# One core, a hybrid decoder layer: weight sums split in place, an earlier norm of the convolution group, a later compression of the values, another order of the last rows

## The chip, the cores and the metric

One core of a Trainium2 chip runs the kernel in one launch. The metric is device time in microseconds: of the kernel before three runs took 1395.77 in the median (1395.15 to 1396.4). Everything read from a trace comes from one profiled execution of 1392.82 us, whose span from the first to the last instruction is 1390.9 us.

## The reference

The layer is one block of a decoder with 1024 tokens, width 1024, all in float32:

```python
n1 = rms_norm(h, g_mix); proj = n1 @ w_in          # columns: conv (3 x 512), q, 6 x k/v, gates
y_conv = b_gate * causal_dwconv(c_gate * x_in, w)  # width-3 convolution, 512 channels
kc = compress_kv(k_cmp); vc = compress_kv(v_cmp)   # blocks of 32 tokens, step 16: silu(flat @ w1) @ w2
y_attn = native_sparse_attention(...)              # compressed + top-8 selected blocks + window of 512, gated
mixed = concat([rms_norm(y_conv, g_gn_conv), rms_norm(y_attn, g_gn_attn)])
h = h + mixed @ w_out
u = causal_dwconv(rms_norm(h, g_ffn) @ w_up, w_ffn_conv)   # 2 x 2816 columns, width 3
h = h + (silu(u_gate) * u_val) @ w_down
h = h + sigmoid(rms_norm(h, g_ple) @ w_ple_gate) * (p @ w_ple_proj)
out = rms_norm(h, g_final)
```

## The kernel before

Activations lie transposed, channels on the partitions and tokens along the free dimension, in tiles of 128 x 1024 called pages (29 of them in the pool). Each float32 operand of a product is split into a high and a low part of type fp32r (split, L99: ACT copies the high part, DVE subtracts for the low part), and each product is three matmuls (mm3, L196 to L199): high with high, high with low, low with high. An operand whose raw data lie in the tile of its low part is split by in_place (L110).

The code is written as generators and loops, and a planner of the framework gives each engine its order: by its own estimate of the times it takes, on each engine, the first instruction in the order of the code that is ready. `behind(later, earlier)` (L203) adds an order between two instructions of one engine without a wait. Tiles are slots of pools; a tile's first writer waits for the last reader of the slot's former tile. Loads are issued from SP's queue, in order.

Weights are named in a list by `plan` (L137; the list is at L289 to L318). `fetch` loads them ahead into raw tiles and `send` splits them; `weights(key)` returns the parts and splits three more ahead. Until the end of attention there are two raw slots (NWR) and eight part slots (NWT), that is four split tiles.

The stages in order:

1. Input products (from L366), the rotary pairs of keys, then the compression: `cmp_proj` makes the 128 columns of the compressed keys (kind 0) and values (kind 1), `stack` (L452) lays them out by transfers from tile to tile, and `compress(kind)` (L464) does 16 x 3 small products with w1, a Silu with a bias, a split, and the product with w2. `queries(g)` (L514) makes two query tiles of 96 matmuls altogether and can call a function between them. L527 to L532: stack of the keys, queries(0), compress of the keys, stack of the values, queries(1) with the compress of the values between its two tiles. Then the values and gates of the eight token tiles (L547 to L554), with the weights vg0, vg3, vg6.
2. The convolution group (L873 to L900) and its sum of squares `cacc`.
3. Attention by blocks of 128 queries, in the order 3, 7, 6, 5, 4, 2, 1, 0 (L954 to L977). `merge` (L837) deals the steps of several generators out over each other: `selected`, `values`, `finish` for the block, `nearest`, `choose`, `window` for the next. The products of the convolution group with its rows of w_out are filled in between (`conv_out`, L846; 16 half tiles of 12 matmuls, three, five and six of them in blocks 2, 1, 0). For them ych, ycl are the split of yc times its gain; the rstd row crb multiplies the product on DVE (L856), and POOL adds this to a page with x, loaded at L851. `attn_norm(hf)` (L909) norms 512 tokens of the attention group; for the upper half it runs as a whole behind the first merge of block 1.
4. `out_half` (L1006): products of the attention group with w_out for the upper and the lower half, and sums of squares. The rstd of the upper half (norm1, L1100) is taken behind three steps of the lower half.
5. The gated MLP by a scheme of seven products in place of eight: the operands are quarters of the weights and of the activations and sums of them. `up_weights(j)` (L1027) loads the two raw tiles of step j (gate and value columns), and makes the parts: products 1 and 2 use the gate columns, products 6 and 5 their sums t (ut), products 7 and 3 the sums a7 and a3 (us), product 4 a part of the value columns (uv). For the steps 0, 1, 20 and 21 (SUMMED) the sums were made in DRAM during attention, as usum, and are loaded: t into a page, a7 and a3 into two tiles of 512. The parts and raw tiles of this stage lie in a pool of 18 slots ("fp"), opened when attention's pools close. Between the halves and the MLP the embeddings' products (`embed`, L1111) and the splits of the moving operands (`moving`, L1063) run.
6. The down products, the gate of the embeddings, and the end: tokens 0 to 767 stay transposed; `final` (L1385) norms them by a rstd whose sums are a small product, and stores them from POOL's queue. The last two token tiles (`late`, 6 and 7) are turned round and computed in rows: `token_product` and `gated` (L1458), which also multiplies by g_final, and `norm` (L1477), which scales by the rstd, half on DVE and half on ACT, and stores. `rsqrt` (L233) is a root on ACT and a reciprocal on DVE, or, for the names in NEWTON, an iteration of twelve small DVE operations.

Of the kernel before, what the change touches and what calls it, by code (L numbers as in the profile page):

```python
# [9 lines left out]
F32 = mybir.dt.float32  # L10
# [26 lines left out]
def hybrid_layer(ctx: ExitStack, tc: tile.TileContext, xT, pT, w_in, w_vg, w_out, w_up, w_down,  # L37
# [157 lines left out]

    def mm3(ps, wh, wl, mh, ml, start, stop, **more):  # L196
        first = nc.tensor.matmul(ps, wh, mh, start=start, stop=False, **more)  # L197
        nc.tensor.matmul(ps, wh, ml, start=False, stop=False, **more)  # L198
        return first, nc.tensor.matmul(ps, wl, mh, start=False, stop=stop, **more)  # L199
# [33 lines left out]
    def rsqrt(ms, n, name, eng=None):  # L233
# [3 lines left out]
        if name not in NEWTON:  # L237
            rs = small.tile([P, 32], F32, tag="rr", name=name + "rr", bufs=1)[:, 0:f]
            nc.scalar.activation(rs, ms, AF.Sqrt, bias=eps, scale=1.0 / n)
# [53 lines left out]
    plan("c11", c_w1[1], 16 * HD)  # L293
    plan_in(7)
    for a in range(0, KC, 3):
        n = min(3, KC - a) * 280
        plan(f"vg{a}", w_vg[:, a * 280:a * 280 + n], n)
    for j in range(4):
# [165 lines left out]
    def compress(kind, st):  # L464
# [20 lines left out]
        split(w2, w2h, w2l, lo_eng="dve")  # L485
        po = bank(n + "o")
        if kind == 0:
            for q in range(2):
                sl = slice(q * P, (q + 1) * P)
                mm3(po[:, sl], w2h[:, sl], w2l[:, sl], hh, hl, True, True)  # L490
# [14 lines left out]
        else:  # L505
            mm3(po[:, 0:64], hh, hl, w2h[:, 0:64], w2l[:, 0:64], True, True)
            for g in range(NG):
                r = slice(64 * g, 64 * g + 64)
                nc.vector.tensor_copy(vc[r, g, :], po[r, 0:64])

# [3 lines left out]
    def queries(g, between=None):  # L514
        ps = []
        for q in range(2):
            t = pair(f"q{g}{q}")
            proj(weights(f"in{4 + 2 * g + q}"), xm, both(t))
            ps.append(t)
            if between and q == 0:  # L520
                between()
# [8 lines left out]
    compress(0, kst)  # L530
    vst = stack(1, *vc_parts)
    queries(1, lambda: compress(1, vst))  # L532
    cmp_stack.close()
    halves = mix.enter_context(tc.tile_pool(name="halves", bufs=1, side="right"))
# [12 lines left out]
    for i in range(NI):  # L547
        sl = slice(i * P, (i + 1) * P)
        pv = bank(f"pv{i}")
        for k in range(KC):  # L550
            mm3(pv[:, 0:280], xh[k][:, sl], xl[k][:, sl], wvh[k], wvl[k], k == 0, k == KC - 1)
        nc.scalar.activation(vsw[i // 4][:, i % 4, :], pv[:, 0:256], AF.Copy, scale=rstd[:, i:i + 1])
        nc.scalar.activation(gates[:, i], pv[:, 256:280].rearrange("p (h b) -> p h b", b=3), AF.Sigmoid,
                             scale=rstd[:, i:i + 1])  # L554

# [290 lines left out]
    def conv_out():  # L846

        for c in range(KC):
# [3 lines left out]
            for hf in range(2):  # L852
                po = bank(f"oc{c}{hf}")
                proj(w, (ch, cl), lambda _: po, (hf,))
                v = half([P, 512], f"ov{c}{hf}")
                nc.vector.tensor_mul(v, po, crb[:, hs(hf)])  # L856
                nc.gpsimd.tensor_add(t[:, hs(hf)], v, t[:, hs(hf)])
# [51 lines left out]
    def attn_norm(hf, sums=None):  # L909
# [17 lines left out]
        yield  # L927
# [712 lines left out]
```

## Time and profile before

| | us |
|---|---|
| median of three runs | 1395.77 |
| the profiled execution | 1392.82 |
| its span | 1390.9 |
| PE busy | 1342.0 (96%) |
| DVE busy | 949.8 (68%) |
| ACT busy | 640.6 (46%) |
| POOL busy | 209.9 (15%) |
| mean granted TensorE clock | 0.989 |

PE is TensorE's matmul row, DVE VectorE, ACT ScalarE, POOL GpSimd, SP the engine that issues loads. The chain of work that ended last is PE for 87% of the span and DVE for 6%. The granted clock is a share of 2.4 GHz: 1.00 is that, 0.50 is 1.2 GHz. A wait is told with the engine and operation that released it; a release by several is put down to the one that came last.

### The profile page before, as it was taken

What the parts mean: (1) busy time and instruction counts of PE and PEld (TensorE: products, weight loads), DVE (VectorE), ACT (ScalarE), POOL (GpSimd) and SP (SyncE); (2) the same over time, 40 slices, a digit from 0 to 9 for tenths busy, and PEclk for the clock granted to TensorE, in tenths of its full rate; (3) what the DMA queues carried; (4) which work ended last, traced back from release to release, by engine and by line L of the source; (5) the groups of instructions that cost most, each with busy time, mean ns of one, the idle gap of its engine ahead of it and who ended that gap; (6) DMA issues with size and microseconds to landing.
All of it is one profiled execution on the core that took longest, in us unless ns stands there. A gap on an engine that the chain in (4) does not pass through costs nothing.

```text
span 1390.9 us, 17780 instructions
## 1 busy us (share of the span) xinstructions
PE 1342.0 (96%) x6395; PEld 1056.3 (76%) x6395; DVE 949.8 (68%) x1754; ACT 640.6 (46%) x1095; POOL 209.9 (15%) x226
## 2 busy tenths in 40 slices
PE   8989999999999999898999999999999999999995
PEld 6869888865666667686888878888887888888884
DVE  7752333387778785787877788876678776566677
ACT  6222111177767652555434444443345564345443
POOL 0211001233333555000010111110001000000001
PEclk9999999999999999999999999999999999999998
DMA  8473311068787971652376667766568996552434
GB/s 274 106 189 120 104 46 46 20 168 162 175 175 156 258 176 39 212 182 83 106 167 157 179 180 180 176 136 136 139 159 235 321 329 216 174 164 75 145 110 174
DMA packets 105462, 220.74 MB, mean 159 GB/s; under 512 B 9120, under 2 KB 30624, under 8 KB 105376
## 3 DMA queue, kind: packets, MB, share of 16 engines
q1 hardware_dynamic: 79280, 153.30, 34.4%
q0 software_dynamic: 26096, 66.33, 23.6%
q8 instruction: 50, 0.82, 0.3%
q14 instruction: 36, 0.29, 0.1%
HBM read 184.99 MB, written 91.49 MB: 199 GB/s over the span
## 4 chain that ended last, share of the span: by engine, by line
PE 87%; DVE 6%; DMA 2%; issue 2%; SPq 1%; ACT 1%; POOL 0%; DVEq 0%; ACTq 0%; POOLq 0%
PE ua L197 4%; PE ua L198 4%; PE ua L199 4%; PE uc L197 3%; PE uc L198 3%; PE uc L199 3%; PE sy L781 2%; PE d L197 2%; PE d L199 2%; PE d L198 2%; PE da L198 2%; PE da L199 2%; PE da L197 2%; PE wy L781 2%; PE g L197 2%
## 5 line engine op out<-in xcount | busy, mean ns | idle before, releaser
L108 DVE TENSOR_TENSOR a<-a 128x512 fp32r<-128x512 f32 x77 | 51.8, 687 | 31.8 <-ACT a L105 31.7
L1207 ACT ACTIVATE uc<-xg,vec 128x1024 f32<-128x1024 f32 x22 | 25.3, 1152 | 97.1 <-DVE xg L1200 94.2
L105 ACT ACTIVATE a<-a 128x512 fp32r<-128x512 f32 x77 | 47.5, 627 | 47.3 <-DMA a<-asum 24.6
L105 ACT ACTIVATE in_h<-in_r 128x1024 fp32r<-128x1024 f32 (+1 forms) x20 | 20.7, 1036 | 96.2 <-PE cx L198 30.1
L1200 DVE TENSOR_TENSOR xg<-uc,e 128x512 f32<-128x512 f32 x22 | 15.2, 690 | 63.6 <-PE uc L199 63.5
L733 ACT ACTIVATE ps<-ps,stat 128x512 f32<-128x512 f32 (+7 forms) x64 | 49.1, 770 | 11.6 <-DVE stat L744 11.5
L108 DVE TENSOR_TENSOR down_p<-down_r,down_p 128x512 fp32r<-128x512 f32 x55 | 37.2, 687 | 24.6 <-ACT down_p L105 24.5
L197 PE MATMUL d<-a,down_p 128*128 128x512 f32 x132 | 52.1, 395 | 0.0
L199 PE MATMUL d<-a,down_p 128*128 128x512 f32 x132 | 52.1, 394 | 0.0
L198 PE MATMUL d<-a,down_p 128*128 128x512 f32 x132 | 52.0, 394 | 0.0
L198 PE MATMUL da<-a,down_p 128*128 128x512 f32 x132 | 51.9, 394 | 0.0
L197 PE MATMUL da<-a,down_p 128*128 128x512 f32 x132 | 50.6, 395 | 1.3 <-ACT a L105 1.3
L105 ACT ACTIVATE down_p<-down_r 128x512 fp32r<-128x512 f32 x55 | 34.2, 627 | 37.2 <-PE d L199 14.1
L199 PE MATMUL da<-a,down_p 128*128 128x512 f32 x132 | 51.1, 393 | 0.0
L105 ACT ACTIVATE ugh<-ugr 128x1024 fp32r<-128x1024 f32 x22 | 23.3, 1059 | 59.3 <-DMA ugr<-in_w_up_dram 59.3
L108 DVE TENSOR_TENSOR in_l<-in_r,in_h 128x1024 fp32r<-128x1024 f32 (+2 forms) x22 | 25.0, 1140 | 28.1 <-ACT in_h L105 28.1
L1235 POOL DMA_DIRECT2D asum<-ad x11 | 8.4, 764 | 236.7 <-DMA ad<-uc 236.7
L1392 POOL DMA_DIRECT2D out_dram<-h x8 | 4.4, 554 | 258.4 <-DVE h L1391 258.4
L197 PE MATMUL g<-g,pg_h 128*128 128x256 f32 (+1 forms) x128 | 43.4, 339 | 0.0
L198 PE MATMUL g<-g,pg_h 128*128 128x256 f32 (+1 forms) x128 | 43.2, 337 | 0.0
L199 PE MATMUL g<-g,pg_l 128*128 128x256 f32 (+1 forms) x128 | 43.1, 338 | 0.0
L652 ACT ACTIVATE pw<-pw,stat 128x640 f32<-128x640 f32 (+3 forms) x56 | 38.3, 687 | 10.0 <-DVE stat L706 5.8
(763 smaller groups left out, 4503.3 us busy)
## 6 DMA issues: line engine op xcount, KB each, us to landing
asum<-ad POOLq DMA_DIRECT2D x33, 768.0 KB, 8.6
wsum<-in_w_down_dram POOLq DMA_DIRECT2D x6, 2816.0 KB, 20.9
ugr<-in_w_up_dram SPq DMA_DIRECT2D x22, 512.0 KB, 6.9
ad<-uc SPq DMA_DIRECT2D x22, 512.0 KB, 2.9
a<-asum SPq DMA_DIRECT2D x44, 256.0 KB, 5.7
down_r<-wsum SPq DMA_DIRECT2D x44, 256.0 KB, 3.8
in_r<-in_w_in_dram SPq DMA_DIRECT2D x18, 512.0 KB, 7.0
uvr<-in_w_up_dram SPq DMA_DIRECT2D x18, 512.0 KB, 5.6
```

The costliest lines, as they stand in the source:

```text
L105: nc.scalar.activation(hi, x, AF.Copy)
L108: (nc.gpsimd if (lo_eng or lo_of[0]) == "pool" else nc.vector).tensor_sub(lo, x, f32(hi))
L197: first = nc.tensor.matmul(ps, wh, mh, start=start, stop=False, **more)
L198: nc.tensor.matmul(ps, wh, ml, start=False, stop=False, **more)
L199: return first, nc.tensor.matmul(ps, wl, mh, start=False, stop=stop, **more)
L652: nc.scalar.activation(w[:, :b.nw * P], w[:, :b.nw * P], AF.Exp, bias=b.M_W[:, h:h + 1], scale=-1.0, accum_out=b.D_W[:, h:h + 1])
L733: nc.scalar.activation(w[:, :nk], w[:, :nk], AF.Exp, bias=b.M_S[:, h:h + 1], scale=-1.0, accum_out=b.D_S[:, h:h + 1])
L781: m = nc.tensor.matmul(py[64 * g:64 * g + 64, :], vals(n, g), pts[g], start=n == 0, stop=n == nblk - 1)
L1200: nc.vector.tensor_add(xg[:, hi], c, e2)
L1207: nc.scalar.activation(u, xe[:, 0:S], AF.Copy, scale=col(tap))
L1235: nc.gpsimd.dma_start(d[:, 0:3], three(one))
L1392: nc.gpsimd.dma_start(out[k], o)
```

## The change

Five edits. (A) compress becomes a generator with a pause before its second product, whose first matmul is put behind the newest mm3; the keys' second part comes after the first half of the first tile of queries(1), the values' two parts come in the loop over token tiles, at tiles 2 and 4; c11 moves behind vg in the list of weights; the pool of the compression closes after that loop. (B) The convolution group is multiplied by gain and rstd row ahead of the split, so that its output products are added to x by one DVE operation; attn_norm pauses after each of its four tiles, and the upper half's is dealt out over the first merge of block 0. (C) Four steps of the lower half instead of three stand before the upper half's rstd. (D) Summed up-weights are loaded into the low parts and split in place. (E) The rstd of tokens 0 to 767 is taken behind weight tile 1 instead of 2; both last rows are normed at the end, both by a root on ACT that is put behind the small root that follows the last Sigmoid; row 6 gets gain and rstd in one operation for each half.

```diff
     def mm3(ps, wh, wl, mh, ml, start, stop, **more):
         first = nc.tensor.matmul(ps, wh, mh, start=start, stop=False, **more)
         nc.tensor.matmul(ps, wh, ml, start=False, stop=False, **more)
-        return first, nc.tensor.matmul(ps, wl, mh, start=False, stop=stop, **more)
+        newest[0] = nc.tensor.matmul(ps, wl, mh, start=False, stop=stop, **more)
+        return first, newest[0]
...
-    def rsqrt(ms, n, name, eng=None):
+    def rsqrt(ms, n, name, eng=None, later=None):
...
-            nc.scalar.activation(rs, ms, AF.Sqrt, bias=eps, scale=1.0 / n)
+            root = nc.scalar.activation(rs, ms, AF.Sqrt, bias=eps, scale=1.0 / n)
+            if later:
+                behind(root, later)
...
-    plan("c11", c_w1[1], 16 * HD)
     plan_in(7)
     for a in range(0, KC, 3):
         n = min(3, KC - a) * 280
         plan(f"vg{a}", w_vg[:, a * 280:a * 280 + n], n)
+    plan("c11", c_w1[1], 16 * HD)
...
         split(w2, w2h, w2l, lo_eng="dve")
+        yield
         po = bank(n + "o")
+        after = newest[0]
         if kind == 0:
             for q in range(2):
                 sl = slice(q * P, (q + 1) * P)
-                mm3(po[:, sl], w2h[:, sl], w2l[:, sl], hh, hl, True, True)
+                behind(mm3(po[:, sl], w2h[:, sl], w2l[:, sl], hh, hl, True, True)[0], after)
...
-            mm3(po[:, 0:64], hh, hl, w2h[:, 0:64], w2l[:, 0:64], True, True)
+            behind(mm3(po[:, 0:64], hh, hl, w2h[:, 0:64], w2l[:, 0:64], True, True)[0], after)
...
-            proj(weights(f"in{4 + 2 * g + q}"), xm, both(t))
+            w = weights(f"in{4 + 2 * g + q}")
+            for hf in range(2):
+                proj(w, xm, both(t), (hf,))
+                if between and q == 0 and hf == 0:
+                    between()
             ps.append(t)
-            if between and q == 0:
-                between()
...
-    compress(0, kst)
+    cmp0 = compress(0, kst)
+    next(cmp0)
     vst = stack(1, *vc_parts)
-    queries(1, lambda: compress(1, vst))
-    cmp_stack.close()
+    queries(1, lambda: next(cmp0))
...
         nc.scalar.activation(vsw[i // 4][:, i % 4, :], pv[:, 0:256], AF.Copy, scale=rstd[:, i:i + 1])
+        if i in (2, 4):
+            if i == 2:
+                cmp1 = compress(1, vst)
+            next(cmp1)
...
-                v = half([P, 512], f"ov{c}{hf}")
-                nc.vector.tensor_mul(v, po, crb[:, hs(hf)])
-                nc.gpsimd.tensor_add(t[:, hs(hf)], v, t[:, hs(hf)])
+                nc.vector.tensor_add(t[:, hs(hf)], po, t[:, hs(hf)])
...
             attn[hf].append((t[:, 0], t[:, 1]))
-        yield
+            yield
...
-                split_gain(yc[k], col(V_GNC + k), ch[k], cl[k])
+                nc.vector.scalar_tensor_tensor(yc[k], yc[k], col(V_GNC + k), crb, op0=ALU.mult, op1=ALU.mult)
+                split(yc[k], ch[k], cl[k])
...
-        merge((selected(cur), 9, 0, 1), (values(cur), min(i + 1, 5) + 3, 0, 1), (some(fill, more[0]), more[0], 0, 1))
+        gens = [(selected(cur), 9, 0, 1), (values(cur), min(i + 1, 5) + 3, 0, 1), (some(fill, more[0]), more[0], 0, 1)]
+        merge(*gens, *([(norm1, 4, 0, 1)] if i == 0 else []))
...
         if i == 1:
-            for _ in attn_norm(1):
-                pass
+            norm1 = attn_norm(1)
+            next(norm1)
...
-        t = page([P, S], f"ut{j}")
-        a7, a3 = (opool[0].tile([P, 512], F32, tag="or", name=f"u{q}s{j}", bufs=2) for q in "73")
+        th_, tl_ = (wpage([P, S], f"ut{q}{j}", F32R) for q in "hl")
+        sh_, sl_ = (wpage([P, S], f"us{q}{j}", F32R) for q in "hl")
+        vp = wpage([P, S], f"uv{j}", F32R)
         if j in SUMMED:
-            src = usum[SUMMED[j]]
-            load(t, src[:, 0:S])
-            load(a7, src[:, S:S + 512])
-            load(a3, src[:, S + 512:])
+            for q, (hi, lo) in enumerate(((th_, tl_), (sh_, sl_))):
+                load(f32(lo), usum[SUMMED[j]][:, q * S:q * S + S])
+                in_place(lo, hi)
+            split(v[:, two], vp[:, one], vp[:, two])
...
-    for _ in range(3):
+    for _ in range(4):
         next(half0)
     next(norm1)
...
-            nc.scalar.activation(warm, g[:, 0:1], AF.Sqrt)
+            rooted[0] = nc.scalar.activation(warm, g[:, 0:1], AF.Sqrt)
...
-        nc.vector.tensor_mul(y, y, gfin[:, cs])
+        if i == late[-1]:
+            nc.vector.tensor_mul(y, y, gfin[:, cs])
...
-        rs = rsqrt(rs, D, f"o{i}")
+        rs = rsqrt(rs, D, f"o{i}", later=rooted[0])
+        if i != late[-1]:
+            for a in (hs(0), hs(1)):
+                y = hT[i][:, a]
+                nc.vector.scalar_tensor_tensor(y, y, rs, gfin[:, a], op0=ALU.mult, op1=ALU.mult)
+                load(out2[:, i - late[0], a], y)
+            return
...
-        if kk == 2:
+        if kk == 1:
             next(done)
...
-            if i != late[-1]:
-                norm(i, used[i])
     for _ in done:
         pass
-    norm(late[-1], used[late[-1]])
+    for i in late:
+        norm(i, used[i])
...
-NEWTON = ("cn", "an1", "on", "o6")
+NEWTON = ("cn", "an1", "on")
```

## Rows read from the trace of the kernel before

**Rows 1.** The page, part 1: busy us, share of the span, instructions.
```profile
PE 1342.0 (96%) x6395; PEld 1056.3 (76%) x6395; DVE 949.8 (68%) x1754; ACT 640.6 (46%) x1095; POOL 209.9 (15%) x226
```

**Rows 2.** Waits of PE, whole span: us in total, times, longest.
```profile
PE ua L197 <- ACT uth L105: 6.3, 1, 6.3
PE oc L197 <- ACT ss L586: 3.2, 1, 3.2
PE vcmph L198 <- issue: 3.0, 1, 3.0
...
PE fn1s L268 <- DVE fn1red L263: 1.4, 1, 1.4
PE w0t L791 <- DVE ov L856: 1.3, 1, 1.3
...
PE kcmpo L197 <- ACT kcmphh L105: 1.2, 1, 1.2
PE vcmph L197 <- PE kcmpo L199: 0.9, 1, 0.9
```

**Rows 3.** Timeline of PE, conv products: start, length, [idle before <- releaser].
```profile
523.65 0.80 PE L197 MATMUL oc<-ych,out_h 128*128 128x512 f32 x1 [3.24 <-ACT ss L586]
...
528.38 0.39 PE L199 MATMUL oc<-ych,out_l 128*128 128x512 f32 x1
...
530.28 0.39 PE L199 MATMUL oc<-ych,out_l 128*128 128x512 f32 x1
530.51 0.40 PE L197 MATMUL oc<-ych,out_h 128*128 128x512 f32 x1
```

**Rows 4.** Windows: length, busy PE PEld DVE ACT POOL, clock, DMA, GB/s.
```profile
524.00:528.00 4.00, 4.00 (x10) 3.12 (x10) 0.51 (x1) 0.08 (x1) 3.92 (x9) 0.50 0.00 0
```

**Rows 5.** Timeline of DVE, low parts of conv and attention group.
```profile
463.54 1.30 DVE L128 SCALAR_TENSOR_TENSOR ycl<-yc,vec,ych 128x1024 fp32r<-128x1024 f32 x1
...
514.23 4.06 DVE L108 TENSOR_TENSOR yan<-ya,yan 128x512 fp32r<-128x512 f32 x4
```

**Rows 6.** Timeline of POOL, additions of x to the last conv products.
```profile
554.97 2.99 POOL L857 TENSOR_TENSOR hx<-ov,hx 128x512 f32<-128x512 f32 x2 [4.26 <-DMA hx<-in_xT_dram]
```

**Rows 7.** Waits of SP's queue, 560 to 670.
```profile
SPq L1042 <- DVE m L108: 20.5, 1, 20.5
```

**Rows 8.** Timeline of all engines, summed weights of up-step 1.
```profile
652.92 0.32 SPq L1042 DMA_DIRECT2D ut<-usum  x1
...
657.32 1.06 ACT L105 ACTIVATE uth<-ut 128x1024 fp32r<-128x1024 f32 x1 [5.16 <-DMA ut<-usum]
658.41 1.23 DVE L108 TENSOR_TENSOR utl<-ut,uth 128x1024 fp32r<-128x1024 f32 x1 [5.52 <-ACT uth L105]
658.43 0.80 PE L197 MATMUL ua<-m,uth 128*128 128x512 f32 x1 [6.27 <-ACT uth L105]
...
661.48 0.40 PE L199 MATMUL ua<-m,utl 128*128 128x512 f32 x1
```

**Rows 9.** Timeline of SP and PE, up-step 21.
```profile
1025.06 0.33 SPq L1032 DMA_DIRECT2D ugr<-in_w_up_dram  x1
...
1037.17 0.40 PE L197 MATMUL ua<-m,uth 128*128 128x512 f32 x1
```

**Rows 10.** Timeline of DVE and PE, the last 31 us.
```profile
1360.40 0.94 DVE L263 TENSOR_REDUCE onred<-ontr 128x24 f32<-128x768 f32 x1
...
1363.80 0.30 PE L268 MATMUL ons<-onred,same 128*128 128x24 f32 x2
...
1380.60 1.28 DVE L1474 TENSOR_TENSOR hT<-hT,gfin 128x512 f32<-128x512 f32 x2
...
1382.55 0.14 DVE L245 TENSOR_SCALAR o6nx<-osum 128x1 f32<-128x1 f32 x1
...
1383.71 0.49 DVE L1483 TENSOR_SCALAR hT<-hT,o7rr 128x512 f32<-128x512 f32 x1
...
1385.46 0.49 DVE L1483 TENSOR_SCALAR hT<-hT,o6ny 128x512 f32<-128x512 f32 x1
```

More of the change, by code (lines that the diff above doesn't have):

```diff
@@ L194, in weights @@
         return [[t[:, k * width:(k + 1) * width] for k in range(n)] for t in (hi, lo)]
+    newest = [None]
     def mm3(ps, wh, wl, mh, ml, start, stop, **more):
@@ L529, in hybrid_layer @@
     queries(0)
-    compress(0, kst)
+    cmp0 = compress(0, kst)
+    next(cmp0)
     vst = stack(1, *vc_parts)
-    queries(1, lambda: compress(1, vst))
-    cmp_stack.close()
-    halves = mix.enter_context(tc.tile_pool(name="halves", bufs=1, side="right"))
+    queries(1, lambda: next(cmp0))
     def half(shape, name, dt=F32):
@@ L552, in hybrid_layer @@
         nc.scalar.activation(vsw[i // 4][:, i % 4, :], pv[:, 0:256], AF.Copy, scale=rstd[:, i:i + 1])
+        if i in (2, 4):
+            if i == 2:
+                cmp1 = compress(1, vst)
+            next(cmp1)
         nc.scalar.activation(gates[:, i], pv[:, 256:280].rearrange("p (h b) -> p h b", b=3), AF.Sigmoid,
                              scale=rstd[:, i:i + 1])
+    cmp_stack.close()
+    halves = mix.enter_context(tc.tile_pool(name="halves", bufs=1, side="right"))
     class Block:
@@ L926, in attn_norm @@
             attn[hf].append((t[:, 0], t[:, 1]))
-        yield
+            yield
     attn = {}
@@ L1037, in up_weights @@
         yield
-        t = page([P, S], f"ut{j}")
-        a7, a3 = (opool[0].tile([P, 512], F32, tag="or", name=f"u{q}s{j}", bufs=2) for q in "73")
+        th_, tl_ = (wpage([P, S], f"ut{q}{j}", F32R) for q in "hl")
+        sh_, sl_ = (wpage([P, S], f"us{q}{j}", F32R) for q in "hl")
+        vp = wpage([P, S], f"uv{j}", F32R)
         if j in SUMMED:
-            src = usum[SUMMED[j]]
-            load(t, src[:, 0:S])
-            load(a7, src[:, S:S + 512])
-            load(a3, src[:, S + 512:])
-        else:
+            for q, (hi, lo) in enumerate(((th_, tl_), (sh_, sl_))):
+                load(f32(lo), usum[SUMMED[j]][:, q * S:q * S + S])
+                in_place(lo, hi)
+            split(v[:, two], vp[:, one], vp[:, two])
+        else:
+            t = page([P, S], f"ut{j}")
+            a7, a3 = (opool[0].tile([P, 512], F32, tag="or", name=f"u{q}s{j}", bufs=2) for q in "73")
             nc.vector.tensor_add(t[:, two], v[:, one], v[:, two])
@@ L1049, in up_weights @@
             nc.vector.tensor_add(a3, g[:, two], t[:, one])
-        th_, tl_ = (wpage([P, S], f"ut{q}{j}", F32R) for q in "hl")
-        split(t, th_, tl_)
-        sh_, sl_ = (wpage([P, S], f"us{q}{j}", F32R) for q in "hl")
-        split(a7, sh_[:, one], sl_[:, one])
-        vp = wpage([P, S], f"uv{j}", F32R)
-        split(v[:, two], vp[:, one], vp[:, two])
-        split(a3, sh_[:, two], sl_[:, two])
+            split(t, th_, tl_)
+            split(a7, sh_[:, one], sl_[:, one])
+            split(v[:, two], vp[:, one], vp[:, two])
+            split(a3, sh_[:, two], sl_[:, two])
         ups[j].update({6: (th_[:, one], tl_[:, one]), 5: (th_[:, two], tl_[:, two]), 7: (sh_[:, one], sl_[:, one]),
@@ L1075, in hybrid_layer @@
     next(half1)
-    next(norm0)
+    for _ in norm0:
+        pass
     next(half1)
@@ L1473, in gated @@
             nc.scalar.activation(z, y, AF.Square, accum_out=sq[:, u:u + 1])
-        nc.vector.tensor_mul(y, y, gfin[:, cs])
+        if i == late[-1]:
+            nc.vector.tensor_mul(y, y, gfin[:, cs])
         return u + 1
+    rooted = [None]
     def norm(i, n):
```

## The prediction

> **What bounds the kernel now.** I read the page's busy shares first, then PE's waits, then the granted clock around the longest of them, then the timeline at those places. PE is busy 1342.0 us of 1390.9 [rows 1], and the change adds and removes no matmul. What it can give back is idle time of PE, time in which PE runs at the lower clock after such idle time, and the tail behind the last product. The reader should see in [rows 2] that the idle time is a short list of single waits, each at a named place. Seven of its rows lie in code that the diff touches: 6.3, 3.2, 3.0, 1.4, 1.3, 1.2 and 0.9, together 17.3 us. An idle stretch costs twice: after the 3.24 us wait the clock is granted at 0.50 [rows 4], which is 1.2 GHz, and the products then start 0.43 us apart instead of 0.23 [rows 3].
>
> The profiled execution took 1392.82 us, its span and 1.92 us around it. The median shown is 1395.77, 2.95 above. I sum against the execution and add 2.95 at the end.
>
> **A. Compression.** Before, the keys' second product waits for the hidden values (1.2), and the values' first products stand between two products of the second query group, where they wait for the earlier product (0.9) and then for something that the view calls issue (3.0) [rows 2]. That last place is just behind the stacking transfers of the values' low parts, so I read it as a transfer that has not landed. Afterwards the keys' second product is held behind the first half of a query tile, 24 products x 0.23 = 5.5 us [rows 3]. The values' products come inside the gates' loop, some 20 us later, with two token tiles between their two parts. The work is the same; its weights (c11) are merely loaded and split behind vg instead of in front of in7. The upper bound is 1.2 + 0.9 + 3.0 = 5.1. From below: the third vg tile now needs its slot before the loop begins, and if it is late by as much as the longest wait here, 3.0, then 2.1 stay. A loss would need a longer delay than any weight tile of this stretch shows, so I put the lower end at 0. I take 4.5, near the upper end, because the c11 tile, which holds a slot in front of vg before, no longer does.
>
> **B. Attention's end.** (1) Before, the norm of the upper tokens is issued in one block. Its four low parts alone hold DVE from 514.23 for 4.06 us [rows 5], and right behind stand PE's waits of 1.3 (transposes that need a bank which a DVE product frees) and 3.2 (conv products, whose bank is freed by ACT behind exponentials that wait for DVE) [rows 2]. Then eleven products from 523.65 to 528.38 take 4.73 us instead of 11 x 0.23 = 2.53 [rows 3], so 2.2 of lower clock. Afterwards the block is dealt out over the next block's merge. Bounds 0 and 1.3 + 3.2 + 2.2 = 6.7; DVE still has all of that work in the same 40 us, so I take 4.5, two thirds.
> (2) The convolution group is normed ahead: four more two-input DVE operations of 128x1024, 1.30 each by the row of the same kind and size [rows 5], so 5.2 us of DVE between the rstd and the first conv product. The sixteen products of 128x512 behind become sixteen additions of the same size: nothing. PE had attention products in front of the first conv product and will take some of them meanwhile. Bounds: 0 and -5.2; I take -2.5.
> (3) The addition moves from POOL to DVE, and with it the wait for the load of x. POOL's last one waited 4.26 us for that load [rows 6], and nothing of PE's stood behind POOL there; behind DVE stand the split of the last weights and the lower tokens' norm. A page for the rstd row is free earlier, so the load may start earlier. Bounds 0 and -4.3; I take -0.5. The sixteen POOL additions vanish from an engine that PE does not wait for: nothing.
> Here a rule weighs against the change. The Trainium skill (TensorE: Matmul & The Clock Gate, opening table) gives VectorE a strict first-in first-out queue, and this trace agrees in that rows 2 and 5 show PE waiting for a DVE operation that needs nothing but its turn. By that rule (3) costs the full 4.3 if the load lands no earlier, and the whole sum below would be 3.8 smaller; with the rest of DVE's new work that is the first rival.
>
> **C. Output halves.** One more step of the lower half's products (12 x 0.23 = 2.8 us) goes in front of the sum product of the upper half's norm, which PE waited 1.4 for [rows 2]. It covers it. I take 1.4; bounds 0 and 1.4. What waits for that norm is DVE, with its result needed after another four products or more.
>
> **D. Summed up-weights.** PE waits 6.27 us for the split sums of up-step 1, which its product 6 reads [rows 8]. The load of it was issued at 652.92, because the queue had waited 20.5 us for a page that the last moving operand gives back [rows 7]. Landing to ACT took until 657.32. Afterwards the sums are loaded into the low parts, in the weight pool, and split in place, so that page isn't asked for. The slots in question are given back by step 0's raw weights and by the embedding's products, which PE's order has in front of up-steps 0 and 1, and 4.4 us for the load (652.92 to 657.32) plus 1.06 and 1.23 for the split [rows 8] fit in. With the wait go seven slow products, 658.43 to 661.48, 3.05 us instead of 1.61: 1.4. Bounds 0 and 7.7; I take 7.0, since DVE has moving operands to split till shortly before. The three loads become two, each one 128x1024, and two splits of 512 become one of 1024: about equal. Up-steps 0, 20 and 21 have the same edit with no wait of PE to take away.
>
> **E. Tail.** After PE's last product only DVE and ACT work. (1) The rstd of the other rows starts one step earlier: its input was ready at 1361.3 and its product ran at 1363.80 [rows 10], so up to 2.5 earlier for the eight output operations that precede the tail on DVE. (2) Row 6 loses its iterated root, the stretch from 1382.55 to 1385.46 (2.9 us), for a root on ACT, and two multiplications of 0.64; it gains two operations of the same size as those instead of the scale of 0.49 and ACT's other half. The last scale now belongs to row 7, which in the old order would be ready 1.7 before row 6 (1383.71 against 1385.46). I take 2.5; bounds 0 and 2.5 + 2.9 = 5.4. The last store and its landing move along.
>
> **Sum.** 4.5 + 4.5 - 2.5 - 0.5 + 1.4 + 7.0 + 2.5 = 16.9. 1392.82 - 16.9 = 1375.9, plus 2.95: 1379 us. All upper ends: 5.1 + 6.7 + 1.4 + 7.7 + 5.4 = 26.3, 1369.5.
>
> **Rivals.**
> *DVE takes PE's place as the bound at the end of attention.* For it: DVE gets 5.2 us of new work and a load to wait for where PE already waits for it twice. Against: the norm's block no longer stands in one piece, and one page is free. Then B gives 0 - 5.2 - 4.3 = -9.5 instead of 1.5, the sum is 5.9: 1390 us.
> *The order doesn't do what it says.* A planner places instructions by its own times; the holds on order are written for the compression and the last roots, but not for the split norm or the output rows. For it: the waits in [rows 2] are all places where its times were wrong. Against: three of the moves are held behind a named product. Then A, C and E give nothing (8.4 less): 8.5, 1387 us.
> *Summed weights late at up-steps 20 and 21: slower than before.* The low parts now need their slot at the load, one load and one split (4.4 + 1.06 + 1.23 = 6.7 us) ahead of use. At step 21 the raw weights are issued only at 1025.06, PE takes the first summed product at 1037.17 [rows 9]: 12.1 us, of which 6.7 are needed. It decides against the change once the slot comes free more than 5.4 us later than the raw one. With a slot that comes only when the step before is through, both steps pay up to 6.7 and 1.4 of clock, and step 1 wins nothing: 16.9 - 7.0 - 16.2 = -6.3, 1402 us. Against: these slots are given back one by one as products end.
>
> **How the numbers follow.** The forecast has a chance of 0.65, DVE as the bound 0.17, the order 0.10, the late weights 0.08. I forecast 1379. The range of 1370 to 1390 holds nine tenths of the forecast's own spread and most of the next two; the last lies outside. A measurement of this kernel can tell about 0.2% (2.8 us) from no change. Faster: nearly all of 0.65, and of the next two 0.22 out of 0.27, 0.87. Within 0.2%: what is left of those two, 0.05. Slower: 0.08.
>
> **What would show it.** A: no wait of PE at the compression, and none of over 1 us at the first vg products. B: no clock of 0.50 at the end of attention; the low parts of the upper norm stand apart on DVE; first conv product later than before relative to the rstd row. C: no wait at the upper half's sum product. D: the load of the sums of step 1 issued by about 640, no gap before product 6 of step 1. E: a tail behind the last product some 2.5 us shorter, with row 7 last in it. The prediction is wrong if PE's idle time between 455 and 530 grows, if up-steps 20 or 21 show a new wait, or if step 1's load is still issued behind the last moving operand.

## The result, and the profile after

The changed kernel takes 1384.39 us in the median of four runs (1381.93 to 1386.24), the kernel before beside it 1395.46 (1394.5 to 1396.4): a ratio of 0.992, 95% interval 0.9902 to 0.9937. That is 11.1 us less, where 16.9 were forecast; the time lies in the range of 1370 to 1390. The profiled execution took 1384.71 us, its span is 1382.9; the one of before had 1390.9, so what is read from these two traces sums to 8.0 us and not to 11.1. One of the four runs of the kernel without edit A, below, took 7497 us and is left out; the 1377.6 in later expectations is the median with it. In the changed kernel the helper mm3 stands at L199 to L201, and other lines are shifted by 5 to 20.

The page's part 1, which answers to [rows 1]:

```profile
PE 1340.4 (97%) x6395; PEld 1055.4 (76%) x6395; DVE 952.6 (69%) x1742; ACT 642.0 (46%) x1093; POOL 188.9 (14%) x210
```

PE has the same work and stands idle for 42.5 us of its span instead of 48.9. Its waits over the whole span (us in total, times, longest) answer to [rows 2]:

```profile
PE vcmph L199 <- ACT c_h L105: 6.6, 1, 6.6
...
PE oa L199 <- ACT out_p L105: 4.1, 2, 2.6
PE sy L797 <- DVE s4p L809: 1.9, 1, 1.9
PE da L200 <- DVE a L108: 1.6, 1, 1.6
PE da L199 <- ACT down_p L101: 1.3, 1, 1.3
...
PE vcmppb L478 <- DVE vcmpw1s L449: 1.1, 1, 1.1
```

Of the seven waits that the forecast summed, the large ones at ua and oc, those at fn1s and w0t, and the two small ones at the compression are gone, or turned into others. The seventh, 3.0 us at vcmph, has become the first row: 6.6 us at the same product, now released by the split of its weights. Where that leaves PE is best seen by stretches. These are the windows of before, and below them those of after (length, then busy us of PE, PEld, DVE, ACT and POOL with counts, granted clock, DMA share, GB/s):

```profile
60.00:140.00 80.00, 75.01 (x449) 65.38 (x448) 34.79 (x47) 21.14 (x36) 11.57 (x6) 0.98 0.58 159
440.00:500.00 60.00, 58.74 (x336) 39.29 (x334) 45.22 (x133) 40.90 (x104) 32.55 (x37) 1.00 1.05 235
500.00:620.00 120.00, 108.54 (x506) 83.69 (x505) 88.47 (x166) 52.53 (x107) 27.22 (x30) 0.97 0.46 147
640.00:660.00 20.00, 13.73 (x57) 10.80 (x56) 11.14 (x18) 9.16 (x17) 0.00 (x0) 0.86 0.23 79
1000.00:1080.00 80.00, 78.57 (x337) 62.90 (x336) 57.24 (x80) 37.91 (x54) 9.59 (x9) 1.00 0.80 199
```

```profile
60.00:140.00 80.00, 70.28 (x413) 61.03 (x412) 36.96 (x47) 22.95 (x35) 11.40 (x5) 0.94 0.59 157
440.00:500.00 60.00, 57.98 (x329) 38.66 (x330) 49.29 (x133) 39.47 (x98) 25.18 (x29) 0.97 1.02 234
500.00:620.00 120.00, 114.25 (x543) 88.36 (x542) 92.49 (x184) 59.48 (x124) 13.43 (x22) 0.99 0.53 157
640.00:660.00 20.00, 20.00 (x88) 16.21 (x87) 16.56 (x25) 9.73 (x17) 0.00 (x0) 1.00 0.00 1
1000.00:1080.00 80.00, 75.72 (x323) 60.12 (x322) 60.40 (x82) 40.76 (x56) 8.44 (x8) 1.00 0.84 214
```

PE's idle time is the length less its busy time. It grows by 4.7 us at the compression (60 to 140) and shrinks by 5.7 at the end of attention and the output halves (500 to 620) and by 6.3 at up-step 1 (640 to 660). It also grows by 2.9 where the up-steps end and the down products begin (1000 to 1080), where no term of the sum stood; the third rival had looked there. The tail is shorter: PE's last product ends 13.1 us before the end of the span, before 15.5.

The wait in the first row has its cause on SP and ACT. In the changed kernel these rows (start, length, idle before and releaser) show c11, the raw tile c_r, issued behind the values' stack and all four of the first queries' stores, and split 16 us after its issue has ended:

```profile
101.13 1.47 SPq L535 DMA_DIRECT2D qd<-q0l  x1
102.70 3.09 SPq L159 DMA_DIRECT2D c_r<-in_c_w_dram  x1
...
121.67 1.06 ACT L105 ACTIVATE c_h<-c_r 128x1024 fp32r<-128x1024 f32 x1 [16.22 <-DMA c_r<-in_c_w_dram]
```

Before, the same 512 KB were issued at 73.38 and split at 78.69:

```profile
73.38 0.79 SPq L159 DMA_DIRECT2D c_r<-in_c_w_dram  x1
...
78.69 1.06 ACT L105 ACTIVATE c_h<-c_r 128x1024 fp32r<-128x1024 f32 x1 [14.04 <-DMA c_r<-in_c_w_dram]
```

The same load takes 5.3 us from issue to split in the one place and 19 in the other. The windows of the changed kernel say what the transfers do meanwhile (the last two columns: DMA share and GB/s):

```profile
112.00:116.00 4.00, 4.00 (x33) 3.95 (x31) 0.00 (x0) 0.00 (x0) 0.00 (x0) 1.00 0.26 81
116.00:120.00 4.00, 0.18 (x2) 0.00 (x0) 0.00 (x0) 0.00 (x0) 0.00 (x0) 0.91 0.24 86
...
124.00:128.00 4.00, 3.97 (x35) 3.97 (x36) 4.00 (x2) 0.67 (x1) 2.21 (x1) 0.50 0.20 43
```

From 116 us on PE, DVE and ACT stand still, and a quarter of the DMA engines' time is used. Behind the idle time PE works at a granted clock of 0.50, 1.2 GHz.

### The profile page after: what moved, and what is told of

It reads as the page before. It is cut to its first block, busy times and chain, and to the rows that moved or that the text cites. A ratio compares the mean times of both kernels' runs of the same rounds, so it can differ in the third digit from the quotient of the medians.

```text
span 1382.9 us, 17705 instructions
## 1 busy us (share of the span) xinstructions
PE 1340.4 (97%) x6395; PEld 1055.4 (76%) x6395; DVE 952.6 (69%) x1742; ACT 642.0 (46%) x1093; POOL 188.9 (14%) x210
## 4 chain that ended last, share of the span: by engine, by line
PE 56%; DVE 2%; DMA 2%; ACT 1%; issue 1%; SPq 0%; DVEq 0%; ACTq 0%
PE ua L199 4%; PE ua L200 4%; PE ua L201 4%; PE uc L200 3%; PE uc L201 3%; PE uc L199 3%; PE d L200 2%; PE d L199 2%; PE d L201 2%; PE da L201 2%; PE da L199 2%; PE da L200 2%; PE g L199 2%; PE g L200 2%; PE g L201 2%; PE ud L201 1%
## 5 line engine op out<-in xcount | busy, mean ns | idle before, releaser
L749 ACT ACTIVATE ps<-ps,stat 128x512 f32<-128x512 f32 (+7 forms) x64 | 49.1, 770 | 10.9 <-DVE stat L760 10.8
L199 PE MATMUL d<-a,down_p 128*128 128x512 f32 x132 | 52.0, 394 | 0.0
L201 PE MATMUL d<-a,down_p 128*128 128x512 f32 x132 | 51.9, 393 | 0.0
L199 PE MATMUL da<-a,down_p 128*128 128x512 f32 x132 | 50.7, 395 | 1.3 <-ACT down_p L101 1.3
L201 PE MATMUL da<-a,down_p 128*128 128x512 f32 x132 | 50.6, 396 | 0.6 <-DVE down_p L102 0.6
L199 PE MATMUL g<-g,pg_h 128*128 128x256 f32 (+1 forms) x128 | 43.4, 339 | 0.0
L201 PE MATMUL g<-g,pg_l 128*128 128x256 f32 (+1 forms) x128 | 43.0, 337 | 0.0
```

Source lines behind the costliest of these rows:

```text
L201: newest[0] = nc.tensor.matmul(ps, wl, mh, start=False, stop=stop, **more)
L749: nc.scalar.activation(w[:, :nk], w[:, :nk], AF.Exp, bias=b.M_S[:, h:h + 1], scale=-1.0, accum_out=b.D_S[:, h:h + 1])
```

## The experiments

All kernels were timed beside the kernel before. Each ratio is to that, with its 95% interval. An interval is some 2 us to either side, so a difference of two kernels below is good to some 2.7 us. Single executions differ too: in ten kernels whose code up to the values and gates is the same, the last product there (pv) ends between 140.92 and 143.90 us in the trace.

**The parts of the change alone and undone.** A wholly undone:

```diff
-    cmp0 = compress(0, kst)
-    next(cmp0)
+    compress(0, kst)
     vst = stack(1, *vc_parts)
-    queries(1, lambda: next(cmp0))
+    queries(1, lambda: compress(1, vst))
...
```

> The changed kernel with edit A wholly undone (compression in one piece, c11 between in6 and in7, as before). Theory: A costs 6.2 us net (12.7 us of idle time and slow clock between 60 and 140 us against 6.5 before), so 1378 us, and PE's three waits of before (1.2, 0.9, 3.0) are back. Rival: A's loss is only what stands in that window by chance of this schedule and is paid elsewhere (same work later): within 2 us of 1384.

Measured: 1377.2 us (1375.98 to 1377.93), ratio 0.9869 (0.9854 to 0.9883). The theory holds: A costs 7.2 us. PE's waits in its place are those of before, smaller than A's:

```profile
PE vcmph L198 <- issue: 2.6, 1, 2.6
PE kcmpo L197 <- ACT kcmphh L105: 1.4, 1, 1.4
PE vcmpo L197 <- ACT vcmphh L105: 0.2, 1, 0.2
```

**c11 earlier in the list.**

```diff
     plan_in(7)
+    plan("c11", c_w1[1], 16 * HD)
     for a in range(0, KC, 3):
...
-    plan("c11", c_w1[1], 16 * HD)
```

> The changed kernel (1384.4 us) with one line moved: the values' first compression weights c11 stand between in7 and vg0 in the list, not behind the vg weights. Theory: in the changed kernel the load of c11 is issued at 102.7 us behind the 32- and 64-partition transfers of the stacks and queries, its high part is split only at 121.7, PE waits 6.6 us and then runs at a granted clock of 0.50; idle time and slow clock of 60 to 140 us come to 12.7 us against 6.5 before. With c11 issued directly behind in7 the wait on it and the slow stretch vanish: 8 to 10 us less, 1375 us. Rival 1: any weight that is issued in that stretch is late, and now the last vg weights are: PE waits 3 to 6 us at the first token tiles instead, 1380 to 1384. Rival 2: the load is not the cause (the stack transfers of the values are late themselves): vcmph waits as before, 1384.

Measured: 1387.57 us, 0.9945 (0.9932 to 0.9958). Rival 1 holds, and is worse than it said. c11 is in time, and the last two vg weights are now issued from 103.67 on, behind the same transfers:

```profile
118.26 1.46 ACT L105 ACTIVATE vg_h<-vg_r 128x840 fp32r<-128x840 f32 x2 [17.60 <-DMA vg_r<-in_w_vg_dram]
...
119.21 0.60 PE L199 MATMUL pv<-vg_h,xh 128*128 128x280 f32 x1 [11.53 <-ACT vg_h L105]
```

**c11 ahead of the low parts in SP's queue.** The stores of the first queries' low parts and the stack transfers of the values' low parts are gathered in `lows`, and then:

```diff
             sent_load[0] = load(raw, src)
+            if key == "c11":
+                for st in lows:
+                    behind(st, sent_load[0])
```

> The changed kernel (1384.4 us), the place of c11 in the list as changed, but the low parts of the first queries' stores and of the values' stack are put behind c11's load in SP's queue (an order of issue, no wait). Theory: A loses because c11's load stands behind these transfers of 32 and 64 partitions; issued some 12 us earlier it lands before PE comes to the values' first products (116 us), so the 6.6 us wait and the clock of 0.50 behind it go, and A's window (60 to 140) loses under 5 us instead of 12.7: 1375 to 1377. Rival 1: the transfers that now come last are as late as c11 was (the values' stack, or the pages that the first queries' stores hold): PE waits 4 us or more at vcmph or at q: 1382 or more. Rival 2: the load is early and the split still late, since ACT and DVE have other work there: 1381 to 1384.

Measured: 1380.9 us, 0.9895 (0.988 to 0.991): 3.5 us less than the change, with intervals that just overlap. It is rival 1 by its wait, though 1.1 below that rival's 1382. c11 is issued at 88.62, and PE waits for the stack of the values instead:

```profile
122.89 0.34 PE L203 MATMUL vcmph<-vcmpst,c_h 128*64 128x128 f32 x1 [7.90 <-DMA vcmpst<-vcmpkl]
```

So in three kernels whatever is issued last of this group is in use at 118 to 123 us. It is the group that is slow, not c11; what in it is slow, the landing times say, in the part on the prediction.

**D alone**, on the kernel before (its core):

```diff
+            for q, (hi, lo) in enumerate(((th_, tl_), (sh_, sl_))):
+                load(f32(lo), usum[SUMMED[j]][:, q * S:q * S + S])
+                in_place(lo, hi)
```

> The kernel before (1395.5 us) with edit D alone (summed up-weights loaded into their low parts and split in place). Theory: the 6.3 us wait at product 6 of up-step 1 and the clock behind it go (8.2 us by the windows 640 to 660). If the new waits of the changed kernel at the start of the down products (2.9 us at 1040 to 1080) are D's too, from its slots at steps 20 and 21, they are here as well: 1390; if they are not: 1387. Rival: D gives nothing without the other edits, since the moving operands' split sets the time there: 1394 to 1395.

Measured: 1391.21 us, 0.997 (0.9958 to 0.9981), 4.1 less; nearest the first figure of the theory. The wait at ua is gone and new ones at the down products are there (3.2 us of idle time at 1000 to 1080, before 1.4, in the change 4.3), so these are D's in the main. One wait was not expected: at the upper half's sum product.

```profile
PE fn1s L268 <- DVE fn1red L263: 3.1, 1, 3.1
...
PE da L198 <- DVE a L108: 1.6, 1, 1.6
...
PE da L197 <- ACT down_p L101: 0.9, 1, 0.9
```

The split of the next gate weights, now early on DVE, stands between that norm's transpose and its reduction:

```profile
591.84 0.70 DVE L261 STREAM_TRANSPOSE fn1tr<-facc 128x512 f32<-128x512 f32 x1
592.46 1.18 DVE L108 TENSOR_TENSOR ugl<-ugr,ugh 128x1024 fp32r<-128x1024 f32 x1
593.56 0.68 DVE L263 TENSOR_REDUCE fn1red<-fn1tr 128x16 f32<-128x512 f32 x1
```

**D at up-steps 0 and 1 only**, A undone:

```diff
-        if j in SUMMED:
+        if j in (NF - 2, NF - 1):
+            ...  # t, a7, a3 loaded and split as before
+        elif j in SUMMED:
```

> The changed kernel with edit A undone (1377.6 us when measured) and edit D only at up-steps 0 and 1; steps 20 and 21 load their sums as before. Theory: the 2.9 us of new PE idle time at 1030 to 1080 us (first down products, released by splits on ACT and DVE) come from D at steps 20 and 21, whose low parts hold weight slots earlier; they go: 1375. Rival 1: step 21 was helped as well, so as much is lost at 1000 to 1040: 1377 to 1378. Rival 2: the idle time comes from somewhere else (other order of the down loads once the sums need no page): waits as with D, 1377 to 1378.

Measured: 1373.55 us (1372.36 to 1374.98), 0.9842 (0.9829 to 0.9856): 3.7 less than with D at all four steps, and the fastest kernel here, 10.8 below the change. Its window answers to the last row of those above: PE's idle time at 1000 to 1080 is 0.4 us.

```profile
1000.00:1080.00 80.00, 79.57 (x343) 63.80 (x342) 62.68 (x88) 42.08 (x61) 9.28 (x9) 1.00 0.89 228
```

With D at steps 20 and 21 (A undone) SP's queue waited for the split of an earlier down weight, and issued the third one at 1033.78; here it had done so by 1030.50. Which slot held that split up was not separated.

```profile
SPq L159 <- DVE down_p L102: 15.7, 2, 15.3
```

The next four leave one thing out of this fastest kernel, or add one to it. **Without C** (the loop of three in place of four):

```diff
-    for _ in range(4):
+    for _ in range(3):
```

> The kernel with A undone and D at up-steps 0 and 1 only (1373.6 us), without C: three steps of the lower half stand before the upper half's rstd, as before. Theory: with D the splits of the up-weights move on DVE in front of the sums of that norm (in the kernel before with D alone PE waited 3.1 us there, with a granted clock of 0.69 at 590 to 600), so C is what makes D pay: 4 to 5 us more, 1378. Rival: C is worth only the 1.4 us wait of before: 1375.

Measured: 1376.36 us, 0.9866 (0.9852 to 0.9881): 2.8 more, between the two, and barely clear of the noise. In the traced executions the output halves take 4.4 us longer (first to last product at oa, 55.4 against 51.0), while the value products ahead of them happened to end 2.4 earlier, where C changes nothing. The wait at fn1s is 2.1 us, and 580 to 600 loses clock besides:

```profile
580.00:600.00 20.00, 17.88 (x72) 14.09 (x71) 17.23 (x26) 6.92 (x10) 0.00 (x0) 0.91 0.39 132
```

**Without B1:**

```diff
-            norm1 = attn_norm(1)
-            next(norm1)
+            for _ in attn_norm(1):
+                pass
```

> The kernel with A undone and D at up-steps 0 and 1 only (1373.6 us), without the dealing out of the upper half's norm (B1): it stands in one piece behind the first merge of block 1, as before. Theory: PE's waits of 1.3 (w0t) and 3 (oc) and the clock of 0.50 behind them are back at 514 to 528 us: 5 to 6.7 us more, 1379 to 1380. Rival: without the DVE products and POOL additions of the convolution group (B2 stays) DVE has the room and the waits do not return: 1374 to 1375.

Measured: 1379.2 us, 0.9891 (0.9876 to 0.9905): 5.7 more, in the range of the theory. The wait of 2.5 at oc is back, released by the same ACT operation ss as in [rows 2], with a clock of 0.63 at 524 to 528; that of 1.3 at w0t is not (0.2). In the traced executions 2.9 us are lost between the last value product and the last convolution product, the place of the theory, and there is 1.0 more idle time at 1000 to 1080, which nothing here explains.

```profile
PE oc L197 <- ACT ss L588: 2.5, 1, 2.5
```

**Without B2**, once in the change and once in the fastest kernel:

```diff
-                nc.vector.tensor_add(t[:, hs(hf)], po, t[:, hs(hf)])
+                v = half([P, 512], f"ov{c}{hf}")
+                nc.vector.tensor_mul(v, po, crb[:, hs(hf)])
+                nc.gpsimd.tensor_add(t[:, hs(hf)], v, t[:, hs(hf)])
...
```

> The changed kernel without the norm of the convolution group ahead of its products: gain at the split, rstd row at the output and the addition on POOL, as before; everything else as changed. Theory: the earlier norm costs what PE shows new at 460 to 480 us (waits of 1.9 and 0.9, granted clock 0.91 in the window, together 3.6 us against 1.2 before), so 2.4 us less: 1382. Rival: the sixteen POOL additions and their DVE products also held banks at 500 to 540 us; without the earlier norm waits there return (1.3 at w0t, part of 3.2 at oc): 1386 to 1389.

> The kernel with A undone and D at up-steps 0 and 1 only (1373.6 us), without the norm of the convolution group ahead (B2). Theory: what it costs at 460 to 468 us (waits of 1.9 and 0.9 and a lower clock, some 4 us) it gives back at 500 to 580 (waits of the products for banks that DVE frees through ov: 1 to 2.5 us), so within 2.5 us of 1373.6, rather below. Rival 1: as a cost only, 1370. Rival 2: as a gain, as the changed kernel without it measured (2.9 us more): 1376 to 1377.

Measured: 1387.32 us, 0.9939 (0.9927 to 0.9951), 2.9 more than the change, with intervals that overlap and traced spans that differ by 0.3 us; and 1377.99 us, 0.9874 (0.9858 to 0.989), 4.4 more than the fastest kernel, with intervals that do not overlap. So norming ahead gains in the fastest kernel, and nearest is rival 2; in the change itself the gain is not clear of the noise. What it gains is seen on DVE between 505 and 560 (groups by line and shape: count, busy us, mean ns). First without B2:

```profile
L108 DVE TENSOR_TENSOR out_l<-out_r,out_h 128x512 fp32r<-128x512 f32 x6 | 5.5, 912 | 0.0
L926 DVE SCALAR_TENSOR_TENSOR ya<-ya,vec,an1rb 128x512 f32<-128x512 f32 x4 | 4.5, 1181 | 0.0
L108 DVE TENSOR_TENSOR yan<-ya,yan 128x512 fp32r<-128x512 f32 x4 | 3.7, 951 | 0.0
L231 DVE TENSOR_TENSOR aacc<-aacc,ya01sq 128x512 f32<-128x512 f32 x1 | 1.8, 1789 | 0.0
```

And with it, in the fastest kernel:

```profile
L108 DVE TENSOR_TENSOR out_l<-out_r,out_h 128x512 fp32r<-128x512 f32 x6 | 4.2, 700 | 0.2 <-ACT out_h L105 0.2
L924 DVE SCALAR_TENSOR_TENSOR ya<-ya,vec,an1rb 128x512 f32<-128x512 f32 x4 | 2.7, 743 | 0.0
L108 DVE TENSOR_TENSOR yan<-ya,yan 128x512 fp32r<-128x512 f32 x4 | 2.6, 684 | 0.0
```

The same operations on the same shapes take 1.30, 1.59 and 1.39 times as long without B2, 1.3, 1.8 and 1.1 us more; the addition aacc, 1.79 us there, is 0.68 in the fastest kernel: 5.3 us of DVE in all. Without B2 POOL's additions run beside them; the long aacc begins at 544.82, inside one of them:

```profile
544.39 1.68 POOL L859 TENSOR_TENSOR hx<-ov,hx 128x512 f32<-128x512 f32 x1 [0.31 <-DVE ov L858]
```

Of the 15 operations of the first list seven took over 1 us, and each of the seven overlaps an operation of POOL; none of those in the second list took over 0.8. PE feels it behind: from the last value product to the last convolution product the two kernels take the same (406.6 us without B2, 406.8 with it), but the output halves take 4.6 longer without it (55.6 against 51.0), and PE waits there 5.5 us in all for the split weights out_p, against 2.5. No run changed POOL's additions alone, so that they and no other part of B2 cost PE this time is argued from these rows.

**The norm ahead dealt out, and its copy put first.** With A undone, the four operations were dealt over the second merge of block 4:

```diff
-        merge(*gens)
+        merge(*gens, *([(conv_norm(), 4, 0, 1)] if i == 4 else []))
```

> The changed kernel with edit A undone (1377.6 us), and the four DVE operations that norm the convolution group (5.95 us in one piece at 456 us there) dealt out over the second merge of block 4 instead of standing in one piece ahead of the splits. Theory: the cost of norming ahead is its standing in one piece: PE's wait for s4p (1.9) and the lower clock behind it go: 1374 to 1376. Rival: the row crb comes only at the end of that merge (454.7 us), so the four operations run in one piece again, and at the same place: 1377 to 1378.

Measured: 1378.36 us, 0.9878 (0.9864 to 0.9891): no change, and the rival. The row crb comes last, and the four stand in one piece from 454.7, right behind it, as they did without the dealing. In the fastest kernel an order does what dealing did not:

```diff
+                if k:
+                    behind(m, dve_copy[0])
```

> The kernel with A undone and D at up-steps 0 and 1 only (1373.6 us when measured), with one order more: the second of the four DVE operations that norm the convolution group stands behind the copy s4p that PE waits 1.9 us for. Theory: the cost of norming ahead is that its four operations (5.96 us) stand in front of that copy, which needs 0.68 us and whose data is ready after the first of them; the waits of 1.9 and 0.9 and the clock of 0.6 to 0.8 at 460 to 468 us go, 3 us: 1370 to 1371. Rival: the first convolution products then come later by the copy, or another DVE operation of that stretch takes the place of s4p (w2p, ss): 1373 to 1374.

Measured: 1373.86 us, 0.985 (0.9835 to 0.9865): the same as without it. The wait at sy is gone and 440 to 500 runs at a clock of 1.00 instead of 0.97, with 0.6 us less idle time. But 500 to 620 has 1.9 more idle time, as the rows show, first without the order, then with it:

```profile
500.00:620.00 120.00, 116.60 (x552) 91.32 (x551) 94.43 (x178) 60.10 (x122) 10.50 (x18) 0.97 0.51 158
```

```profile
500.00:620.00 120.00, 114.68 (x546) 89.42 (x545) 94.54 (x179) 59.69 (x120) 9.51 (x16) 0.99 0.53 160
```

The clock is higher there as well, 0.99 against 0.97, so these rows alone do not show a loss. Counted from the last value product, the last convolution product comes 2.1 us sooner with the order (404.7 against 406.8). Then the output halves take 1.2 longer (52.2 against 51.0): PE waits 0.9 at fn1s and 1.1 more at oa for what DVE and ACT split. And 1000 to 1080 has 0.6 more idle time. I take it that the gain was given back there; that these places and no chance of the schedule took it was not tested.

**E alone**, on the kernel before (its core):

```diff
-        if kk == 2:
+        if kk == 1:
...
-    norm(late[-1], used[late[-1]])
+    for i in late:
+        norm(i, used[i])
```

> The kernel before (1395.5 us) with edit E alone (rstd of tokens 0 to 767 one step earlier, both last rows normed at the end with a root on ACT). Theory: the tail behind PE's last product is 2.4 us shorter (13.1 against 15.5), as in the changed kernel: 1393. Rival: the earlier sum product and its rstd row now stand ahead of the gate's work on PE and DVE and cost there what the tail gives: 1395.

Measured: 1393.29 us (eleven runs), 0.9984 (0.9975 to 0.9993): 2.2 less, as the theory has it; in its traced execution the tail is 13.9 us, 1.6 shorter than before. In the changed kernel's tail, which answers to [rows 10], row 7 is last, and its root follows row 6's:

```profile
1376.22 1.41 DVE L1505 SCALAR_TENSOR_TENSOR hT<-hT,o6rr,gfin 128x512 f32<-128x512 f32 x2
1377.99 0.16 DVE L245 RECIPROCAL o7rr<-o7rr 128x1 f32<-128x1 f32 x1 [0.36 <-ACT o7rr L242]
1378.19 0.49 DVE L1509 TENSOR_SCALAR hT<-hT,o7rr 128x512 f32<-128x512 f32 x1
```

## Why the prediction was right in the total and wrong in its terms

Us gained, forecast against measured; what each is worth was taken from the kernel without it, for B1, B2 and C from the fastest kernel, and D is what is left of 11.1. The edits need not add up, so this is a rough account:

| step | forecast | measured | from |
|---|---|---|---|
| A | +4.5 | -7.2 | A undone |
| B1 | +4.5 | +5.7 | without B1 |
| B2 and B3 | -3.0 | +4.4 | without B2 |
| C | +1.4 | +2.8 | without C |
| D | +7.0 | +3.2 | the rest; of it -3.7 at steps 20 and 21 |
| E | +2.5 | +2.2 | E alone |

By this account the total was near because two misses of 11.7 and 3.8 against the change stood beside one of 7.4 in its favour: the range was met by luck, not by its terms. If B2 is put at the 2.9 that it showed in the change itself, D is 4.7; alone it was 4.1.

**A** is the step that failed: "A loss would need a longer delay than any weight tile of this stretch shows, so I put the lower end at 0." Before, the last weight tile that the stretch needs, a vg tile, was issued at 95.14, ahead of the last two of the queries' four stores; the change put one behind all four. I had said that a moved step's load moves too, and priced the slot that it asks for, but not the transfers that it is queued behind. The three orders show that the group ends at about 120 us whatever comes last in it. It did so before as well:

```profile
103.49 8.06 SPq L159 DMA_DIRECT2D in_r<-in_w_in_dram  x2
...
109.75 0.67 ACT L105 ACTIVATE vg_h<-vg_r 128x560 fp32r<-128x560 f32 x1 [4.60 <-DMA vg_r<-in_w_vg_dram]
...
121.28 1.06 ACT L105 ACTIVATE in_h<-in_r 128x1024 fp32r<-128x1024 f32 x1 [10.26 <-DMA in_r<-in_w_in_dram]
```

The vg tile was split 14.6 us after its issue, and the tile issued at 103.49, behind all four stores, after 17.8. So the trace of before had the longer delays that the quoted sentence denies; only c11, issued ahead of the group, took 5.3. PE waited for neither of the two, and so neither showed among its waits.

Why the group is slow is seen in the landing times that the traces keep for each transfer. c11 has sixteen in the changed kernel: twelve parts land at 108.42 to 109.05, 6 us after its issue, and the other four at 118.56, 119.43, 120.58 and 121.58. The queries' store issued just ahead of it, at 101.13, has four late ones, at 117.31, 118.16, 119.34 and 120.35, each 1.2 to 1.3 us ahead of one of c11's. So four DMA engines carry the stores, and a quarter of every load waits behind them there. In the two other orders it is the same: twelve parts of the vg weight issued at 103.67 land by 109.10 and the last at 118.17, twelve of the last stack transfer by 109.16 and the last at 122.80. The DMA share of 0.24 to 0.26 at 112 to 120 is that of 4 engines out of 16. Each of the four stores of a query group writes a target of 4 x 32 x 1024, with the 4 outermost, from 128 partitions. The Trainium skill (DMA: Bandwidth & Descriptors, "Why a DMA increments its semaphore by 16 and not by 1") says that a transfer runs on the largest number of engines up to 16 that divides the outermost dimension of both its sides. By that rule the stores use 4 engines, and the trace agrees, in the four late parts and in the share. Whether a store with its 32 rows outermost would cure it was not tried.

**B2** failed with its sign: "The sixteen POOL additions vanish from an engine that PE does not wait for: nothing." PE does not wait for POOL, but DVE's operations are longer beside it: 5.3 us of DVE between 505 and 560, and with that the split weights of the output halves come later. [rows 5] had the sign of it, yan at 4.06 us for four, 1.02 each, where the fastest kernel's mean is 684 ns. The cost of norming ahead was forecast well where it was looked for: 2.5, against 0.8 us more idle time at 440 to 500 and 0.03 of clock on 60 us, 1.8, together 2.6. The Trainium skill (SBUF — State Buffer, "Who interferes with whom") says that a DVE operation with two inputs in SBUF contends with a GpSimd operation that reads SBUF, and that one with at most one input there, outside the two-port modes, does not. The trace agrees: ov, one of whose inputs lies in PSUM, took 683 ns beside the same additions, and aacc, which reads two SBUF tiles, 1.79 us.

**B3** (the load of x) cost nothing: the changed kernel's additions hx wait for PE alone. The rule of the Trainium skill that the prediction cites there, a strict first-in first-out queue on VectorE, was not the one that counted; the first rival, DVE as the bound at the end of attention, did not come.

**B1 and E** were right in mechanism and within 1.2 us in size. **C** was undersized, as far as the noise lets one say, since it was priced on the wait of before. D puts four splits on DVE in front of the norm that C covers, and without C that wait is 2.1 to 3.1 us: the two edits are worth more together than the sum had them.

**D** was right at step 1: the load of its sums was issued by 595 and PE waits for nothing between 640 and 660, 6.3 us and the clock of 0.86. At steps 20 and 21 the third rival's place was right and its price was not: 3.7 us, and not at the summed products but behind them, at the first down weights, whose loads and splits came later. I had given it a chance as a whole case of 1402 us, not a place in the sum.

Of the signs of being wrong one came, in small: up-step 21 has a new wait of 0.7 us, at 1053.35, released by a copy on ACT (e) and not by a load. PE's idle time between 455 and 530 fell from 6.0 to 2.0 us, and step 1's load came early. Of the signs that were to show the change at work, A's failed: there is a wait at the compression. The change is faster by 0.8%, and no rival came as a whole, though the second rival's 1387 lies nearer to the measured time than the forecast does; C and E, which it puts at nothing, gave what they were to give.

## What to carry to other kernels

When a load moves in a queue, list what it will stand behind and what those transfers reach, not only when its slot is free; a stretch where DMA share stays at a quarter while everything waits, or a load of which a few parts land long after the rest, is a sign that few DMA engines carry the work in front. Taking work off an idle engine can be a gain on a busy one: compare the mean duration of the same operation with and without the other engine beside it. And price edits in pairs where one moves work in front of what another covers.

## What the runs showed of the hardware that was not expected

A DVE operation with two SBUF operands took up to 2.6 times as long while POOL worked on SBUF (aacc 1.79 us against 0.68; ya 1181 ns against 743 in the mean of four), one with an input in PSUM no longer (ov 683 ns). A 512 KB load took 5.3 us from issue to split behind stack transfers of the keys, and 19 behind the values' stack and the queries' stores: twelve of its sixteen parts had landed 6.4 us after the issue, and the other four came behind the four parts of a store, with 81 to 86 GB/s moved in all at 112 to 120.
